# Time mixing in one fixed TensorE order, with the substitution recorded later and the receptance multiplied early

## The chip, the cores and the metric

The kernel runs on one core of a Trainium2 chip. The metric is the device time of one execution in microseconds (us). Each stated time is the median of several runs; beside it stands one profiled execution, from which all rows below come. TensorE (PE) does matrix products and transposes, VectorE (DVE), ScalarE (ACT) and GpSimd (POOL) do the rest, and SyncE (SP) issues the loads of the weights. Each engine works through its own queue in order; semaphores tie the queues together.

## The reference, cut to what matters

The reference is two blocks of two layers each, on 256 tokens of width 1024 in float32. The first block (sparse, latent and forgetting attention, a cross attention and an MLP in each layer) is not touched. A layer of the second block is, cut to its core:

```python
h = rms_norm_2(x, norm_g) * (1.0 + scale) + shift
proj = h @ w_in
pool_u, pool_g, q, k, v, ret_g, rw, rw_g, gate_logits = jnp.split(proj, points, axis=-1)
o_pool = causal_pool_mixer(pool_u, pool_w, pool_scale) * jax.nn.silu(pool_g)
o_ret = retention(q, k, v, positions, ret_norm_g) * jax.nn.silu(ret_g)
o_rwkv = rwkv7_time_mix(rw, ...) * jax.nn.silu(rw_g)
y = jnp.einsum('btnw,nwd->btnd', stack(o_pool, o_ret, o_rwkv), w_branch)
x = x + gate * (jnp.sum(jax.nn.sigmoid(gate_logits) * y, axis=2) @ w_out)
```

In rwkv7_time_mix the projected features are first shifted, p + (p_prev - p) * mu, and then each of eight heads runs a recurrence over the tokens, in which a state of 64 x 64 is multiplied by a decay and corrected by two outer products (time mixing). retention rotates q and k (rotary positions), takes masked and decayed scores in chunks of 128 tokens, and normalises each head.

## The kernel before, in words

A layer of the second block is the function `block2_layer`, called twice; layer 0 begins at about 928 us of the span and layer 1 at about 1281 us. The weights `w_in_2` are cut into chunks of 512 columns. A chunk comes as four loads (tile `raw`, four buffers, issued by SyncE at L76); each is split into a high half `hi` (ScalarE, L112) and a low half `lo` (VectorE, L113), and a raw buffer is free when its low half is done. A gemm does three products for each pair of operand and weight (L138, L139, L140). `gemm_b` writes features by tokens, 24 matmuls of 256 columns for each 128 features; `gemm_a` writes tokens by features with 512 columns.

The stage of time mixing, in the order of the code:

- With the operand that is not yet normalised (`xop`, 258 columns), the low-rank input and the keys `kT` are multiplied (chunk 0); `mixed_unscaled` puts the norm and the token shift in afterwards. Then `hop`, the normalised operand, is made.
- The decays (L1070 to L1085), the squares of the keys (ACT, L1089), their sums by head (PE, L1095), and `kn`, a power on GpSimd (L1098).
- The receptance `rT` (chunk 1) with `hop`, in the function `shifted`; the exponentials `Ei`, `En`, `Ee` out of matmuls at L1106; `Bt` and its companions on VectorE (L1131 to L1144).
- The values `vT` (chunk 2), then masked products (`masked`, L1154, copied by a mask at L1157) into `LT`, which GpSimd writes to memory (`lt`) and reads back as `band`, a 16 x 16 block for each of 128 rows.
- The substitution (L1185, L1186): fifteen products and fifteen reduces on VectorE, which solve these blocks into `zb`; a DMA from GpSimd's queue writes them to memory (`zd`, L1187).
- `bonus`, then `rotated(4)` and `rotated(3)`, the retention's keys `rk_` and queries `rq` (chunks 4 and 3). Each is two gemms of 48 matmuls, and for each of its four pieces two copies on ScalarE into `row` (three buffers, L1382, L1383), a product with the cosine on VectorE (L1386), and a product with the sine and an addition on GpSimd (L1384, L1387).
- The retention's values `rv` (chunk 5), `inverse_parts` (four loads of `zd` into `TT` from GpSimd's queue, L1195), `silu_gate` for chunk 6 into `kT` (L1369, L1370), the retention's scores (PE L1412 and L1417, VectorE L1414 and L1420) and its output (PE L1429, L1432).
- `recurrence` (it inverts the blocks, L1202, and solves) interleaved with `other_branches`, which are the pooling branch, the remaining gates and one of the branch gates.

Outside of two sections with a manual schedule for PE, a scheduler sets the order of an engine's instructions from the order in which they are recorded and from their dependences. Inside such a section (L1515) TensorE's order is that of the code. The generators `recurrence` and `other_branches` are advanced by turns there, so that each yield is a place at which the other's matmuls go in. PSUM tiles have tags with fixed numbers of banks: "mm" four, "s" two, "t" and "o" one each. `bt("gt", ...)` has four buffers, "P" and "PT" four; `raw_load` takes a raw buffer, `aux` a "gt" buffer.

Of the kernel before, what the change touches and what calls it, by code (L numbers as in the profile page):

```python
# [42 lines left out]
def program(ctx: ExitStack, tc: tile.TileContext, T: dict, out: bass.AP):  # L43
# [939 lines left out]
    def block2_layer(l, x, r, us, K, xop):  # L983
# [61 lines left out]
        for j in range(4):  # L1045
            mixed_unscaled(kT[:, j, :], ups[1 + j], 1 + j)

# [52 lines left out]
        us = chunk_b(1)  # L1100
        shifted(1, rT, us)
# [73 lines left out]
        zb = bt("PT", [128, 31, 16])  # L1175
        pool.memset(zb, 0.0)
        pool.memset(zb[:, 15:31, 0:1], 1.0)
        tmp = bt("dg", [128, 256])
        zrow = zb[:, 15:31, :]
        for i in range(14, -1, -1):  # L1180
            m = 15 - i
            zv = bass.AP(tensor=zrow.tensor, offset=zrow.offset + 16 * i + 15 + 1,
                         ap=[list(zrow.ap[0]), [1, m], [15, m]])
            tv = tmp[:, :m * m].rearrange("p (a b) -> p a b", b=m)
            ver.tensor_mul(out=tv, in0=zv, in1=band[:, i, 1:m + 1].unsqueeze(1).broadcast_to([128, m, m]))  # L1185
            ver.reduce_sum(out=zrow[:, i, 1:m + 1], in_=tv, axis=AX.X)  # L1186
        pool.dma_start(out=flat(K["zd"], 16, *blocks), in_=zrow)  # L1187

# [45 lines left out]
        def bonus():  # L1234

            for n in range(2):
                p = pst("t")
                for ct in range(4):
                    pe.transpose(p[:, 128 * ct:128 * ct + 128], vT[:, ct, tok(n)], ident)
                ver.tensor_copy(out=Vn[:, n, :], in_=p)  # L1240
            for c2 in range(2):
                p = pst("s")
                for i in range(2):
                    pe.matmul(p[:, 256 * i:256 * i + 256], lhsT=K["bones"], rhs=kT[:, 2 * c2 + i, :],
                              start=True, stop=True)
                ver.tensor_mul(out=flat2(vT[:, 2 * c2:2 * c2 + 2, :]), in0=p, in1=flat2(vT[:, 2 * c2:2 * c2 + 2, :]))

        def by_token():
            BK = bt("aT", [128, 2, 512])
            for i, src in enumerate((Bt, Kt)):  # L1250
                p = pst("t")
                for ct in range(4):
                    pe.transpose(p[:, 128 * ct:128 * ct + 128], src[:, ct, 0:128], ident)
                act.copy(out=BK[:, i], in_=p)
            return BK[:, 0], BK[:, 1]
# [134 lines left out]
        bonus()  # L1390
        rk_ = rotated(4)
        pool.tensor_mul(out=Ei, in0=Ei, in1=rT)

        rq = rotated(3)
        rv = bt("gt", [128, 2, 512])
        us = chunk(5)
        o = [pst("mm"), pst("mm")]
        gemm_a(o, hop, us)
        for t in range(2):
            ver.tensor_copy(out=rv[:, t, :], in_=o[t])  # L1400

        inverse_parts()
        oop = Op([None, None, None])
        sg = {}

        def retention_scores():
            dm = raw_load(T["ret_decay"]).rearrange("p (h t) -> p h t", t=256)
            sc0 = bt("gt", [128, 4, 256])
# [10 lines left out]
            sc1 = bt("gt", [128, 4, 128])  # L1419
# [30 lines left out]
        def other_branches(on):  # L1450
# [21 lines left out]
            w0 = raw_load(T["pool_band"][0]).rearrange("p (g t) -> p g t", t=256)  # L1472
# [24 lines left out]
            th[0, 0] = bt("gt", [128, 4, 256])  # L1497
            yield from gate_tanh(th[0, 0], 0, 0)
# [12 lines left out]
        sg[6] = bt("kT", [128, 4, 256])  # L1511
        for _ in silu_gate(sg[6], 6):
            pass
        on = retention_out(*retention_scores())
        with tc.manual_schedule(engines={mybir.EngineType.PE}):  # L1515
            others = other_branches(on)
            for _ in recurrence():
# [368 lines left out]
```

## Time and profile before

| what | value |
| --- | --- |
| median of 3 runs | 1629.22 us (1626.84 to 1631.49) |
| profiled execution | 1626.35 us |
| its span | 1624.6 us |
| mean granted TensorE clock | 0.979 |
| TensorE busy | 1555.3 us, 96% |
| VectorE, ScalarE, GpSimd busy | 1104.6, 741.3, 252.3 us |

The profiled execution lies 2.9 us under the median. A row of busy time counts an engine as busy from an instruction's start to its end, and matmuls overlap. A wait is idle time of an engine and is put down to the instruction that ended it. [...]

### The profile page before, as it was taken

Reading aid. Unit: us, or ns where it says so; the run is one execution under the profiler, and the core shown is the slowest. Engines: PE = TensorE matmul, PEld = TensorE weight load, DVE = VectorE, ACT = ScalarE, POOL = GpSimd, SP = SyncE. Lnnn points to the kernel's source line nnn. Section 1 sums busy time; section 2 is a strip of 40 time slices with the busy share of each in tenths; the row PEclk is TensorE's granted clock in tenths of the full one; section 3 lists DMA queues with packets and bytes.
Section 4 is the critical chain, followed back from the end, with each engine's and each line's share of the span. In section 5 each row is a group of like instructions: output and inputs, shape, how many; then the busy total and the mean of one; then the engine's idle time right before and its main releaser. Section 6 shows DMA issues by size and latency. Waiting matters only on the chain.

```text
span 1624.6 us, 29823 instructions
## 1 busy us (share of the span) xinstructions
PE 1555.3 (96%) x12106; PEld 1433.0 (88%) x12106; DVE 1104.6 (68%) x1773; ACT 741.3 (46%) x1190; POOL 252.3 (16%) x247
## 2 busy tenths in 40 slices
PE   7999999999999999998999999899999999899998
PEld 6789997899879899987999789789999889799997
DVE  5476568866776766689876777765565786664754
ACT  4666344544445664454544364423443654233441
POOL 1000110111100001101111132311111313101202
PEclk9899999999999999999999989999999999999999
DMA  8733465687776234664788645624365346432552
GB/s 294 256 105 114 159 230 173 201 274 256 259 254 207 93 105 155 209 211 144 257 274 269 215 134 160 196 85 132 104 183 181 104 159 175 148 130 79 176 184 69
DMA packets 81033, 288.98 MB, mean 178 GB/s; under 512 B 9224, under 2 KB 10304, under 8 KB 80896
## 3 DMA queue, kind: packets, MB, share of 16 engines
q1 hardware_dynamic: 78768, 280.07, 52.6%
q0 software_dynamic: 2128, 7.01, 1.5%
q8 instruction: 95, 1.56, 0.4%
q14 instruction: 42, 0.34, 0.1%
HBM read 281.48 MB, written 5.55 MB: 177 GB/s over the span
## 4 chain that ended last, share of the span: by engine, by line
PE 42%; DVE 6%; DMA 2%; ACT 2%; issue 2%; POOL 1%; DVEq 0%; POOLq 0%; ACTq 0%
PE mm L138 10%; PE mm L139 10%; PE mm L140 10%; DVE lo L113 2%; PE s L138 2%; PE s L139 2%; PE s L140 2%; DMA raw<-in_w_in 1%; PE s L1154 1%; ACT hi L112 1%; PE o L1270 1%; PE t L1270 1%; PE o L1301 1%; PE t L1202 1%; PE s L1202 0%
## 5 line engine op out<-in xcount | busy, mean ns | idle before, releaser
L113 DVE TENSOR_TENSOR lo<-raw,hi 128x1024 fp32r<-128x1024 f32 (+1 forms) x429 | 545.6, 1279 | 258.1 <-ACT hi L112 256.1
L112 ACT CAST hi<-raw 128x1024 fp32r<-128x1024 f32 (+1 forms) x435 | 453.0, 1048 | 518.8 <-PE mm L139 238.0
L138 PE MATMUL mm<-act,hi 128*128 128x256 f32 x1808 | 522.2, 289 | 2.0 <-DVE act L130 2.0
L139 PE MATMUL mm<-act,hi 128*128 128x256 f32 x1808 | 514.2, 285 | 0.5 <-DVE act L128 0.5
L140 PE MATMUL mm<-act,lo 128*128 128x256 f32 x1808 | 513.6, 285 | 0.0
L138 PEld LDWEIGHTS mm<-act,hi 128*128 128x128 f32 x1808 | 348.5, 193 | 8.8 <-issue 4.3
L139 PEld LDWEIGHTS mm<-act,hi 128*128 128x128 f32 x1808 | 348.4, 193 | 1.9 <-DVE act L128 0.9
L140 PEld LDWEIGHTS mm<-act,lo 128*128 128x128 f32 x1808 | 347.7, 193 | 0.5 <-issue 0.2
L138 PE MATMUL mm<-hi,act 128*128 128x512 f32 (+1 forms) x320 | 126.2, 395 | 5.4 <-ACT hi L127 5.2
L138 PE MATMUL s<-act,hi 128*128 128x256 f32 x448 | 127.8, 285 | 3.3 <-DVE P L128 1.7
L140 PE MATMUL s<-act,lo 128*128 128x256 f32 x448 | 127.5, 285 | 0.0
L139 PE MATMUL s<-act,hi 128*128 128x256 f32 x448 | 127.5, 285 | 0.0
L140 PE MATMUL mm<-hi,act 128*128 128x512 f32 (+1 forms) x320 | 123.8, 387 | 3.0 <-DVE act L128 3.0
L139 PE MATMUL mm<-lo,act 128*128 128x512 f32 (+1 forms) x320 | 123.6, 386 | 0.4 <-DVE lo L113 0.4
L138 PEld LDWEIGHTS s<-act,hi 128*128 128x128 f32 x448 | 86.7, 194 | 4.4 <-DVE P L128 2.2
L139 PEld LDWEIGHTS s<-act,hi 128*128 128x128 f32 x448 | 86.6, 193 | 0.2
L140 PEld LDWEIGHTS s<-act,lo 128*128 128x128 f32 x448 | 86.7, 194 | 0.0
L138 PEld LDWEIGHTS mm<-hi,act 128*128 128x128 f32 x320 | 61.4, 192 | 18.1 <-ACT hi L127 5.2
L1623 DVE CUSTOM_DVE_ANT_0 raw<-raw,gt 128x1024 f32<-128x1024 f32 x48 | 59.9, 1253 | 25.4 <-DMA raw<-in_w_ada 25.3
L140 PEld LDWEIGHTS mm<-hi,act 128*128 128x128 f32 x320 | 61.2, 191 | 17.0 <-DVE act L128 4.3
L138 PE MATMUL mm<-hi,P 128*128 128x512 f32 x192 | 74.8, 389 | 0.0
L139 PE MATMUL mm<-lo,P 128*128 128x512 f32 x192 | 74.8, 389 | 0.0
(509 smaller groups left out, 2324.8 us busy)
## 6 DMA issues: line engine op xcount, KB each, us to landing
raw<-in_w_in SPq DMA_DIRECT2D x119, 512.0 KB, 4.6
raw<-in_w_up SPq DMA_DIRECT2D x64, 512.0 KB, 4.6
raw<-in_w_down SPq DMA_DIRECT2D x64, 512.0 KB, 4.6
raw<-in_w_gate SPq DMA_DIRECT2D x48, 512.0 KB, 3.5
raw<-in_w_ada SPq DMA_DIRECT2D x48, 512.0 KB, 4.4
raw<-in_w_gl SPq DMA_DIRECT2D x48, 512.0 KB, 3.5
raw<-in_w_branch SPq DMA_DIRECT2D x24, 512.0 KB, 3.4
raw<-in_w_br SPq DMA_DIRECT2D x16, 512.0 KB, 3.4
```

Of the source, the lines that this page charges most:

```text
L112: act.copy(out=h[:, :cols], in_=r[:, :cols])
L113: (eng or ver).tensor_sub(out=l[:, :cols], in0=r[:, :cols], in1=h.bitcast(F32)[:, :cols])
L138: pe.matmul(o, lhsT=lh, rhs=rh, start=first, stop=False)
L139: pe.matmul(o, lhsT=lh, rhs=rl, start=False, stop=False)
L140: pe.matmul(o, lhsT=ll, rhs=rh, start=False, stop=last)
L1154: pe.matmul(p[par][:, 128 * ct:128 * ct + 128], lhsT=lm[pp, ct, cs], rhs=rm[pp, ct, cs], start=True, stop=True)
L1202: pe.matmul(p[half(a), 64 * i:64 * i + 64], lhsT=lhs(i, a), rhs=rhs(i, a), start=True, stop=True)
L1270: pe.matmul(p[par][:, 64 * ct:64 * ct + 64], lhsT=m[par][:, ct, :], rhs=v(par, ct), start=first and ct == 0, stop=last and ct == 3, skip_g ...
L1301: pe.matmul(p[half(a), col_of(par, ct)], lhsT=TT[n][half(a), 4 * par + ct, :], rhs=x0[half(a), col_of(par, ct)], start=True, stop=True)
L1623: ver.tensor_tensor_reduce(out=r, in0=r, in1=box["c"], scale=1.0, scalar=0.0, op0=ALU.mult, op1=ALU.add, accum_out=mods[l][:, o:o + 1])
```

## The change

First, the receptance's gemm (chunk 1) is moved up behind the keys' gemm and uses the operand `xop`; `mixed_unscaled` finishes it at the old place. Second, the manual section begins earlier: it now holds `rv`, `bonus`, `rotated(4)`, the substitution, `rotated(3)`, `inverse_parts`, the gate of chunk 6 in two halves around the scores, the retention's output, four steps of `other_branches`, and only then the recurrence. `other_branches` ends with three branch gates instead of one; the two later ones used to follow the section. Third, the transposes in `bonus` and `by_token` alternate between the banks "t" and "o", the copies of `Vn` go to ScalarE, and `ret_decay` and the first half of `pool_band` come through `aux`.

```diff
@@ -1044,6 +1044,11 @@
             mixed_unscaled(kT[:, j, :], ups[1 + j], 1 + j)
+        us = chunk_b(1)
+        ups = []
+        for j in range(4):
+            ups.append(pst("mm"))
+            gemm_b(ups[j][:, 0:258], xop, us, 128 * j)
...
@@ -1097,8 +1102,8 @@
-        us = chunk_b(1)
-        shifted(1, rT, us)
+        for j in range(4):
+            mixed_unscaled(rT[:, j, :], ups[j], 5 + j)
...
@@ -1172,20 +1177,6 @@
         pool.dma_start(out=band, in_=flat(K["lt"], 0, *blocks))
-        zb = bt("PT", [128, 31, 16])
...
-        pool.dma_start(out=flat(K["zd"], 16, *blocks), in_=zrow)
...
@@ -1234,10 +1225,10 @@
-                p = pst("t")
+                p = pst("to"[n])
...
-                ver.tensor_copy(out=Vn[:, n, :], in_=p)
+                act.copy(out=Vn[:, n, :], in_=p)
...
@@ -1387,25 +1378,11 @@
-        bonus()
-        rk_ = rotated(4)
-        pool.tensor_mul(out=Ei, in0=Ei, in1=rT)
-
-        rq = rotated(3)
-        rv = bt("gt", [128, 2, 512])
...
-        inverse_parts()
...
-            dm = raw_load(T["ret_decay"]).rearrange("p (h t) -> p h t", t=256)
-            sc0 = bt("gt", [128, 4, 256])
+            sc0 = bt("P", [128, 4, 256])
...
@@ -1494,8 +1471,9 @@
-            th[0, 0] = bt("gt", [128, 4, 256])
-            yield from gate_tanh(th[0, 0], 0, 0)
+            for br in range(3):
+                th[0, br] = bt("gt", [128, 4, 256])
+                yield from gate_tanh(th[0, br], 0, br)
...
@@ -1508,12 +1486,43 @@
-        sg[6] = bt("kT", [128, 4, 256])
-        for _ in silu_gate(sg[6], 6):
-            pass
-        on = retention_out(*retention_scores())
         with tc.manual_schedule(engines={mybir.EngineType.PE}):
+            rv = bt("gt", [128, 2, 512])
+            us = chunk(5)
+            o = [pst("mm"), pst("mm")]
+            gemm_a(o, hop, us)
+            for t in range(2):
+                ver.tensor_copy(out=rv[:, t, :], in_=o[t])
+            bonus()
+            rk_ = rotated(4)
+            pool.tensor_mul(out=Ei, in0=Ei, in1=rT)
+            zb = bt("PT", [128, 31, 16])
...
+            pool.dma_start(out=flat(K["zd"], 16, *blocks), in_=zrow)
+            rq = rotated(3)
+            dm = aux(T["ret_decay"]).rearrange("p (h t) -> p h t", t=256)
+            inverse_parts()
+            sg[6] = bt("kT", [128, 4, 256])
+            gate = silu_gate(sg[6], 6)
+            for _ in range(2):
+                next(gate)
+            scs = retention_scores()
+            for _ in gate:
+                pass
+            on = retention_out(*scs)
             others = other_branches(on)
+            for _ in range(4):
+                next(others)
             for _ in recurrence():
                 next(others, None)
```

In the orders below each line of the kernel keeps its own number, so that one statement has two: L1384 and L1387 (the two GpSimd pieces of `rotated`) are L1375 and L1378 in the changed kernel, L1382 and L1383 (its copies) L1373 and L1374, L1187 (zd) L1511, L1195 (TT) L1186, L1412 and L1417 (scores) L1389 and L1394, L1095 L1100, L1106 L1111, L1154 L1159, L1343 L1334.

The queue of GpSimd around zd in layer 0, before; the last two products and additions belong to the second half of rq:

```order
L1384 TENSOR_TENSOR row_10622<-row_10622,sin 128x256
L1387 TENSOR_TENSOR gt_10566<-gt_10566,row_10622 128x256
L1187 DMA zd<-PT_10335 2048x1x16
L1384 TENSOR_TENSOR row_10677<-row_10677,sin 128x256
L1195 DMA TT_10370<-zd 64x8x64
L1387 TENSOR_TENSOR gt_10566<-gt_10566,row_10677 128x256
L1384 TENSOR_TENSOR row_10683<-row_10683,sin 128x256
L1195 DMA TT_10370<-zd 64x8x64
L1387 TENSOR_TENSOR gt_10566<-gt_10566,row_10683 128x256
L1195 DMA TT_10371<-zd 64x8x64 x2
```

The same place in the changed kernel, where gt_10665 is rq:

```order
L1378 TENSOR_TENSOR gt_10482<-gt_10482,row_10599 128x256
L1511 DMA zd<-PT_10606 2048x1x16
L1186 DMA TT_10355<-zd 64x8x64
L1375 TENSOR_TENSOR row_10715<-row_10715,sin 128x256
L1186 DMA TT_10355<-zd 64x8x64
L1378 TENSOR_TENSOR gt_10665<-gt_10665,row_10715 128x256
L1375 TENSOR_TENSOR row_10721<-row_10721,sin 128x256
L1186 DMA TT_10356<-zd 64x8x64
L1378 TENSOR_TENSOR gt_10665<-gt_10665,row_10721 128x256
L1186 DMA TT_10356<-zd 64x8x64
L1375 TENSOR_TENSOR row_10776<-row_10776,sin 128x256
L1378 TENSOR_TENSOR gt_10665<-gt_10665,row_10776 128x256
```

All eight pieces of rq now stand behind zd and the first TT load, where three stood behind the first TT load before.

ScalarE's queue in layer 1, before, from rq's last copies (row) to the casts of gate 6 (hi_2462 and later; hi_2433 and hi_2436 are rv's):

```order
L1382 COPY row_2408_14405<-mm_2407_14356 64x256
L1383 COPY row_2408_14405<-mm_2407_14356 64x256
L1382 COPY row_2409_14411<-mm_2407_14356 64x256
L1383 COPY row_2409_14411<-mm_2407_14356 64x256
L112 CAST hi_2433_14513<-raw_2432_14511 128x1024
L112 CAST hi_2436_14519<-raw_2435_14517 128x1024
L112 CAST hi_2462_14736<-raw_2461_14734 128x1024
L112 CAST hi_2465_14742<-raw_2464_14740 128x1024
L112 CAST hi_2468_14748<-raw_2467_14746 128x1024
```

The same place in the changed kernel, where hi_2444 to hi_2453 are the four units of gate 6:

```order
L1373 COPY row_2437_14469<-mm_2435_14414 64x256
L1374 COPY row_2437_14469<-mm_2435_14414 64x256
L112 CAST hi_2444_14545<-raw_2443_14543 128x1024
L1373 COPY row_2439_14524<-mm_2438_14475 64x256
L1374 COPY row_2439_14524<-mm_2438_14475 64x256
L112 CAST hi_2447_14551<-raw_2446_14549 128x1024
L1373 COPY row_2440_14530<-mm_2438_14475 64x256
L1374 COPY row_2440_14530<-mm_2438_14475 64x256
L112 CAST hi_2450_14557<-raw_2449_14555 128x1024
L112 CAST hi_2453_14563<-raw_2452_14561 128x1024
```

The casts of gate 6 now stand between and behind the last copies of rq; row_2439 takes the buffer of row_2419, the last of rk's four rows, whose sine product and addition on GpSimd stand behind a TT load.

TensorE's queue in layer 1, before, at the scores, from the last matmuls of rv's and gate 6's gemms on (here the second half of gate 6, mm_2439, and then the retention's output):

```order
L138 MATMUL mm_2439_14574<-act_2292_13629,hi_2436_14519 128x256
L139 MATMUL mm_2439_14574<-act_2293_13630,hi_2436_14519 128x256
L140 MATMUL mm_2439_14574<-act_2292_13629,lo_2437_14520 128x256
L1412 MATMUL mm_2442_14628<-gt_2403_14294,gt_2384_14146 128x256 x2
L1412 MATMUL mm_2443_14632<-gt_2403_14294,gt_2384_14146 128x256 x2
L1417 MATMUL mm_2444_14636<-gt_2403_14294,gt_2384_14146 128x128 x4
L1429 MATMUL mm_2447_14644<-gt_2410_14417,gt_2441_14627 128x128 x4
```

The same place in the changed kernel, where mm_2455 is the first half of gate 6 and mm_2461 the second:

```order
L138 MATMUL mm_2455_14567<-act_2316_13773,hi_2447_14551 128x256
L139 MATMUL mm_2455_14567<-act_2317_13774,hi_2447_14551 128x256
L140 MATMUL mm_2455_14567<-act_2316_13773,lo_2448_14552 128x256
L1389 MATMUL mm_2457_14617<-gt_2434_14413,gt_2413_14230 128x256 x2
L1389 MATMUL mm_2458_14621<-gt_2434_14413,gt_2413_14230 128x256 x2
L1394 MATMUL mm_2459_14625<-gt_2434_14413,gt_2413_14230 128x128 x4
L138 MATMUL mm_2461_14634<-act_2314_13771,hi_2450_14557 128x256
L139 MATMUL mm_2461_14634<-act_2315_13772,hi_2450_14557 128x256
```

The scores now stand between the two halves of gate 6, 48 matmuls behind rq's gemm; before, rv's gemm and the whole of gate 6 stood between.

## Rows read from the trace of the kernel before

**Rows 1.** The page, busy time of each engine over the whole span.

```profile
PE 1555.3 (96%) x12106; PEld 1433.0 (88%) x12106; DVE 1104.6 (68%) x1773; ACT 741.3 (46%) x1190; POOL 252.3 (16%) x247
```

**Rows 2.** Waits of PE from 928 us on: total us, times, longest.

```profile
engine line waited for: us in total, times, longest us
PE mm L1417 <- DVE kT L1370: 8.9, 2, 5.1
PE t L1343 <- DVE PT L1336: 3.9, 2, 1.9
PE t L1239 <- DVE vT L1006: 2.2, 3, 1.1
...
PE mm L1429 <- DVE gt L1414: 2.2, 1, 2.2
PE t L1095 <- ACT P L1089: 2.1, 1, 2.1
```

**Rows 3.** Busy time and granted clock (PEclk) of five stretches.

```profile
core 0: us, PE busy (x) PEld busy (x) DVE busy (x) ACT busy (x) POOL busy (x), PEclk, DMA share, GB/s
956.60:966.80 10.20, 10.20 (x36) 8.15 (x36) 6.45 (x10) 7.10 (x12) 3.16 (x2) 0.50 0.24 67
...
1052.10:1059.00 6.90, 5.07 (x22) 4.79 (x23) 5.73 (x13) 1.54 (x2) 0.00 (x0) 0.51 0.64 208
...
1390.20:1396.90 6.70, 5.22 (x22) 4.91 (x23) 6.64 (x12) 2.59 (x3) 0.00 (x0) 0.50 0.65 201
...
1161.40:1164.80 3.40, 3.40 (x18) 3.40 (x17) 1.30 (x1) 2.39 (x6) 2.19 (x1) 0.50 0.00 0
...
1295.00:1305.00 10.00, 9.93 (x61) 7.80 (x60) 8.72 (x20) 6.88 (x15) 3.64 (x3) 1.00 0.04 6
```

**Rows 4.** PE in order of time: first matmuls of rv and gate 6, scores, tail.

```profile
start us, us, engine line op out<-in xcount [idle before <-releaser]
1022.51 0.40 PE L138 MATMUL mm<-hi,act 128*128 128x512 f32 x1
...
1160.36 0.63 PE L1343 MATMUL t<-cpack,PT 128*128 128x128 f32 x4 [1.93 <-DVE PT L1336]
...
1361.77 0.40 PE L138 MATMUL mm<-hi,act 128*128 128x512 f32 x1
...
1372.68 0.28 PE L138 MATMUL mm<-act,hi 128*128 128x256 f32 x1
...
1384.52 1.97 PE L1412 MATMUL mm<-gt,gt 128*128 128x256 f32 x8 [0.17 <-DVE gt L1400]
```

**Rows 5.** Waits of SP's DMA queue, 1335 to 1400 us: total us, times, longest.

```profile
SPq L76 <- DVE PT L1186: 16.2, 2, 11.1
```

**Rows 6.** POOL in order of time, layer 0, columns as in rows 4.

```profile
1031.09 1.13 POOL L1187 DMA_DIRECT2D zd<-PT  x1 [0.17 <-issue]
...
1039.87 0.72 POOL L1195 DMA_DIRECT2D TT<-zd  x1 [6.13 <-DMA zd<-PT]
1040.59 0.76 POOL L1387 TENSOR_TENSOR gt<-gt,row 128x256 f32<-128x256 f32 x1
```

**Rows 7.** DVE in order of time, layer 0: masked copies, substitution, low half, splitting.

```profile
998.40 1.34 DVE L1157 COPY_PREDICATED P<-masks,s 128x512 f32<-128x512 uint8 x2
...
1012.10 0.16 DVE L1185 TENSOR_TENSOR dg<-PT,dg 128x1 f32<-128x1 f32 x1 [5.45 <-DMA dg<-lt]
...
1030.40 0.39 DVE L1186 TENSOR_REDUCE PT<-dg 128x15 f32<-128x225 f32 x1
...
1042.10 1.23 DVE L113 TENSOR_TENSOR lo<-raw,hi 128x1024 fp32r<-128x1024 f32 x1 [4.33 <-ACT hi L112]
...
1168.97 1.23 DVE L131 SCALAR_TENSOR_TENSOR act<-rT,act 128x1024 fp32r<-128x1024 f32 x1
```

**Rows 8.** POOL in order of time, layer 1.

```profile
1363.80 1.55 POOL L1384 TENSOR_TENSOR row<-row,sin 128x256 f32<-128x256 f32 x1 [1.20 <-ACT row L1383]
...
1370.05 1.14 POOL L1187 DMA_DIRECT2D zd<-PT  x1 [0.28 <-issue]
1379.11 0.72 POOL L1195 DMA_DIRECT2D TT<-zd  x1 [7.92 <-DMA zd<-PT]
```

**Rows 9.** ACT in order of time, layer 1: a cast of gate 6.

```profile
1385.01 1.05 ACT L112 CAST hi<-raw 128x1024 fp32r<-128x1024 f32 x1 [1.12 <-DMA raw<-in_w_in]
```

More of the change, by code (lines that the diff above doesn't have):

```diff
@@ L1174, in block2_layer @@
         pool.dma_start(out=band, in_=flat(K["lt"], 0, *blocks))
-        zb = bt("PT", [128, 31, 16])
[L1176 to L1186, printed above, removed]
-        pool.dma_start(out=flat(K["zd"], 16, *blocks), in_=zrow)
         TT = [bt("TT", [128, 8, 64]) for n in range(2)]
@@ L1250, in by_token @@
             for i, src in enumerate((Bt, Kt)):
-                p = pst("t")
+                p = pst("to"[i])
                 for ct in range(4):
@@ L1388, in rotated @@
             return dst
-        bonus()
-        rk_ = rotated(4)
-        pool.tensor_mul(out=Ei, in0=Ei, in1=rT)
-        rq = rotated(3)
-        rv = bt("gt", [128, 2, 512])
[L1396 to L1400, printed above, removed]
-        inverse_parts()
         oop = Op([None, None, None])
@@ L1418, in retention_scores @@
                           start=True, stop=True)
-            sc1 = bt("gt", [128, 4, 128])
+            sc1 = bt("PT", [128, 4, 128])
             ver.tensor_mul(out=sc1, in0=p.rearrange("p (a b) -> p a b", b=128), in1=dm[:, :, 0:128])
@@ L1471, in other_branches @@
                     yield
-            w0 = raw_load(T["pool_band"][0]).rearrange("p (g t) -> p g t", t=256)
+            w0 = aux(T["pool_band"][0]).rearrange("p (g t) -> p g t", t=256)
             w1 = raw_load(T["pool_band"][1])[:, 0:512].rearrange("p (g t) -> p g t", t=128)
@@ L1509, in gate_tanh @@
                 act.activation(out=flat2(tt[:, j:j + 2, :]), in_=p, func=AF.Tanh, scale=0.5)
-        sg[6] = bt("kT", [128, 4, 256])
-        for _ in silu_gate(sg[6], 6):
-            pass
-        on = retention_out(*retention_scores())
         with tc.manual_schedule(engines={mybir.EngineType.PE}):
+            rv = bt("gt", [128, 2, 512])
[8 more added lines that the diff above has]
+            zb = bt("PT", [128, 31, 16])
+            pool.memset(zb, 0.0)
+            pool.memset(zb[:, 15:31, 0:1], 1.0)
+            tmp = bt("dg", [128, 256])
+            zrow = zb[:, 15:31, :]
+            for i in range(14, -1, -1):
+                m = 15 - i
+                zv = bass.AP(tensor=zrow.tensor, offset=zrow.offset + 16 * i + 15 + 1,
+                             ap=[list(zrow.ap[0]), [1, m], [15, m]])
+                tv = tmp[:, :m * m].rearrange("p (a b) -> p a b", b=m)
+                ver.tensor_mul(out=tv, in0=zv, in1=band[:, i, 1:m + 1].unsqueeze(1).broadcast_to([128, m, m]))
+                ver.reduce_sum(out=zrow[:, i, 1:m + 1], in_=tv, axis=AX.X)
+            pool.dma_start(out=flat(K["zd"], 16, *blocks), in_=zrow)
[10 more added lines that the diff above has]
+            on = retention_out(*scs)
             others = other_branches(on)
+            for _ in range(4):
+                next(others)
             for _ in recurrence():
```

## The prediction

> **What bounds the kernel now.** I read the busy times first, then the list of what TensorE waited for, then the granted clock of the stretches behind the waits, and last the order of time on the engines that release TensorE. TensorE is busy 96% of the span [rows 1], and the change leaves its matmuls what they are. So what can be won is the idle time of TensorE and the stretches at half clock, and both only in the second block, from 928 us on, where the changed function runs twice (layer 0, then layer 1). Here is what is lost there now:
>
> - Ahead of L1095, once, 2.1 us: the squares of the keys (ACT, L1089) come late [rows 2]. Behind it 10.2 us run at clock 0.50 with TensorE busy throughout [rows 3]. [...] In layer 1 there is no such wait, and the same lines run at clock 1.00 [rows 3].
> - L1239 behind vT: 2.2 us, of which 1.4 in layer 1 [rows 2].
> - L1417 waits for gate 6 (kT): 8.9 us in two waits, 5.1 of it in layer 1, so 3.8 in layer 0; L1429 2.2 us in layer 0 [rows 2]. Behind them the clock is 0.51 and 0.50, with 5.1 and 5.2 us of busy time [rows 3]: 2.5 and 2.6 us lost. The source is the order on VectorE. SyncE's weight loads wait 16.2 us in layer 1 for the substitution's reduces, because the low halves (L113) that free the four raw buffers are queued behind them [rows 5]; ScalarE's cast of gate 6 then waits for the landing [rows 9], kT is late, and TensorE stands the 5.1 us.
> - L1343 waits 3.9 us in two waits [rows 2], with 3.4 us at clock 0.50 behind one of them [rows 3], 1.7 us lost each time.
>
> In sum 2.1 + 5.1 + 0.8 + 3.8 + 2.2 + 2.5 + 1.9 + 1.7 = 20.1 us in layer 0 and 1.4 + 5.1 + 2.6 + 2.0 + 1.7 = 12.8 us in layer 1.
>
> **The change, part by part.**
>
> *Receptance early.* Its four gemms of 24 matmuls stay the same work (258 columns instead of 256). Ahead of L1100 (old L1095) they put some 11.5 us of TensorE work, since a chunk of 96 such matmuls takes as long as gate 6 does, 1372.7 to 1384.4 [rows 4]. The missing squares need 2.1 us: the wait goes, and with it the fall of the clock, 7.2 us in layer 0 and nothing in layer 1. In exchange the exponentials' matmuls (L1111) lose the cover of this gemm, and eight of them come with few gemm matmuls between. I charge 1.0 us in each layer; from below that is 0, from above the 2.1 us of the wait that goes. VectorE gets eight small operations more and GpSimd four; they lie under the gemm.
>
> *Substitution after rotated(4).* On VectorE the low halves of rk now stand ahead of the substitution, and those of the first half of gate 6 get their raw buffers from them. The late weights behind L1417 go, and with them what stands at L1417 and L1429 with its clock. But zd's DMA now stands ahead of all GpSimd work of rq (layer 0), or ahead of that and the second half of rk's (layer 1), and the TT loads are queued right behind it; each L1375 and L1378 of rq stands behind a TT load that waits for zd. Before, four of rq's eight pieces were done when zd was issued in layer 0, and rv's gemm of 10.9 us and gate 6's 11.6 us [rows 4] stood between rq and its first reader, L1412. Now the first reader, L1389, stands half a gate behind rq, 5.8 us. This is the price of the change.
>
> *Layer 0 step by step.* The masked copies ended at 999.7 and the substitution began at 1012.1 [rows 7]. With 7.2 us won, 1.0 lost and six rv matmuls now ahead of L1159 they end about 5 us sooner, so the substitution begins at 1007. It took 18.7 us, to 1030.8 [rows 7], with other work between; with less of that I take 17, to 1024. zd was issued at 1031.1 and GpSimd went on at 1039.9 [rows 6]: 8.8 us, so TT starts at 1032.8. Then follow four TT issues of 0.7 us and eight pieces of 0.75 us [rows 6], 8.8 us, to 1041.6. TensorE finished rq at 1022.5 [rows 4]; less 7.2 + 0.8 us, plus 10.9 of rv, that is 1025.4, and with 0.4 of the new small waits about 1026. VectorE is still in the substitution then, so gate 6's low half comes some 1.3 us late, and TensorE stands at L1389 at 1033 instead of going on. It ends L1389 at 1042, of which about 0.5 is work: a wait of 8.5 to 9 us, take 9. Behind it the clock will be at half as behind L1417 now: 2.5 us. Sum of the new costs: 1.0 + 1.3 + 9 + 2.5 = 13.8 us.
>
> *Layer 1 step by step.* Nothing is won ahead of the masks, so the substitution begins at 1352 and ends at 1370 as before (its zd was issued at 1370.1 and let GpSimd go on at 1379.1 [rows 8]). After that come TT, the last L1375 of rk, TT and its L1378, 2.9 us, to 1382. For that L1378 waits the third copy of rq (L1373, it takes over the buffer of rk's last row), and behind this copy on ScalarE stands the cast of the second weight unit of gate 6: two copies, a cast of 1.05 us [rows 9], a low half of 1.2 us [rows 7], to 1384.4 and 1385.6. TensorE finished rq at 1361.8 [rows 4]; less 1.4, plus 10.9 and 1.0, that is 1372.3, and after twelve matmuls of gate 6, at 1373.7, it stands: 10.7 to 11 us. Behind it the remaining 36 matmuls run at half clock, 2.5 us. GpSimd's last piece of rq ends about 1390, under these. Sum: 1.0 + 11 + 2.5 = 14.5 us.
>
> *The tail.* Ahead of L1334 (old L1343) stand 48 gate matmuls where 30 stood; at 0.12 us each (11.6 us for 96 [rows 4]) that is 2.2 us more cover against waits of 1.9 and 2.0 us: the wait goes with its clock, 3.6 us in each layer. What is late next is the branch gemm that needs yT; two gate halves and two branch gemms, 11.5 us, lie between, and the chain through the addition and the splitting took 9.2 us (1161.0 to 1170.2 [rows 4, 7]). I charge nothing; without that cover it would be 1 to 3 us.
>
> *Alternating banks and copies on ScalarE, decay by the other pool.* Small waits of the order of 0.7 us (bonus, by_token) go, 1.4 us in all.
>
> Sum: 20.1 + 12.8 + 1.4 - 13.8 - 14.5 = 6.0 us won. The profiled execution took 1626.35 us, so 1620.3; the median of the runs shown lies 2.9 us above the profiled execution, so **1623 us**, 0.4% faster.
>
> [...] zd takes 8.8 us from issue to GpSimd's release in layer 0 and 9.0 in layer 1 [rows 6, 8]. [...]
>
> **Rivals.**
> - *Short wait for zd.* [...] Chance 0.12. [...]
> - *The queue costs nothing*, as GpSimd is through with rq's pieces before TensorE asks. Then 31 us are won (34.3 less the small waits): 1598 us. The order on GpSimd and the landings speak against it. Chance 0.12.
> - *The clock behind the masks falls anyway*, because the small matmuls at L1075 to L1100 draw it down without any wait. Then the 5.1 us stay: 1628 us, no change. Layer 1's clock of 1.00 at these lines [rows 3] speaks against it. Chance 0.14.
> - *Slower: GpSimd's pieces stretched.* The pieces that stand behind zd take 0.75 us when VectorE is idle or slow, but 1.55 us in the one row here that stands beside its work [rows 8], and it will work: it does the low halves that had to wait. Sixteen pieces at 1.55 are 12.8 us more, and the clock then stays low as long as the longest stretch seen, 10.2 us, 2.5 us more in each layer: 1623 + 17.8 = 1641 us. It turns the sign from a mean piece of about 1.1 us on (6 us over sixteen pieces). Against it: most rows show 0.74 to 0.76. Chance 0.14.
>
> **How the numbers follow.** My forecast has 0.48; around it the wait for zd and the start of the substitution are uncertain by some 3 us in each layer, so it spreads over 1615 to 1631. About 0.3% (4.9 us) is what a measurement of this kernel can tell from no change. Faster: 0.31 of the forecast's 0.48, the first two rivals' 0.24, 0.02 of the third: 0.57. Slower: 0.13 of the last, 0.01 of the forecast and 0.02 of the third: 0.16. Same: the rest, 0.27. The range, 1600 to 1636, leaves out most of the 1598 and 1641 cases.
>
> **What would show it.** Right: no wait at L1100, clock 1.0 at 955 to 970, GpSimd still for 6 to 8 us ahead of the first TT load in both layers, TensorE waiting about 9 us at L1389 in layer 0 and about 11 us at the second weight unit of gate 6 (released by the cast) in layer 1, nothing at L1334. Wrong: a wait of less than 4 us in either place, TensorE waiting over 3 us at L1111 or at the branch gemm, or a clock below 1 behind L1075.

## The result and the profile after

The changed kernel takes 1617.54 us (median of 6 runs, 1615.14 to 1623.85) against 1629.15 us (6 runs, 1626.78 to 1631.49): a ratio of 0.9943, with an interval of 0.9921 to 0.9965. It is faster by 0.6%. The forecast was 1623, its range 1600 to 1636. The profiled execution took 1615.78 us (before 1626.35), its span is 1613.7 us (before 1624.6) and its mean granted clock 0.983 (before 0.979).

The span is 10.9 us shorter. Measured between the starts of the waits at L356 and at L1023, layer 0 went from 355.97 to 347.86 us, 8.1 less; from there to the end, layer 1 went from 339.58 to 338.03, 1.5 less. The remaining 1.2 us lie in the first block, which has the same code; the six runs of the changed kernel lie up to 8.7 us apart.

The busy times answer to [rows 1]; TensorE is busy 6.1 us less, though it does the same 12106 matmuls, because at a mean granted clock of 0.983 instead of 0.979 fewer of them ran at half clock:

```profile
PE 1549.2 (96%) x12106; PEld 1428.4 (89%) x12106; DVE 1101.8 (68%) x1785; ACT 742.8 (46%) x1194; POOL 260.0 (16%) x255
```

What TensorE waited for from 926 us on (total us, times, longest), against [rows 2]. The waits at L1095, L1239, L1343, L1417 and L1429 have no successor; these rows are new but the last, which was at 0.4 us (L1154):

```profile
PE mm L138 <- ACT hi L112: 5.2, 3, 4.1
PE mm L1389 <- POOL gt L1378: 4.6, 2, 2.9
PE mm L140 <- DVE lo L113: 3.4, 3, 1.9
...
PE s L1159 <- DVE LT L1162: 1.8, 2, 1.5
...
PE s L1159 <- DVE Bt L1142: 1.5, 1, 1.5
```

Busy time and granted clock of five stretches, columns as in [rows 3]:

```profile
955.00:968.80 13.80, 13.80 (x93) 11.51 (x92) 11.23 (x27) 9.20 (x16) 4.86 (x7) 1.00 0.49 176
968.90:972.20 3.30, 3.30 (x11) 2.85 (x12) 1.12 (x3) 2.15 (x4) 2.14 (x2) 0.50 0.46 159
1040.60:1047.30 6.70, 5.00 (x21) 4.61 (x21) 4.17 (x7) 2.09 (x2) 1.78 (x2) 0.50 0.49 153
1303.40:1310.10 6.70, 6.70 (x19) 5.12 (x18) 1.67 (x3) 3.20 (x8) 2.15 (x1) 0.50 0.42 151
1371.70:1378.40 6.70, 3.94 (x16) 3.64 (x17) 6.06 (x5) 4.50 (x6) 6.53 (x7) 0.50 0.43 127
```

The third and the fifth stretch stand behind the waits at L1389 and in gate 6, as foreseen. The second and the fourth do not: at 968.9 and 1303.4 TensorE is busy for the whole stretch, 3.30 of 3.30 and 6.70 of 6.70 us, and has not stood still ahead of it (no idle time over 0.15 us between 934 and 987 us, nor between 1278 and 1326), yet the granted clock is 0.50, half of full speed.

GpSimd in layer 0 from zd on (start, duration, idle time before), against [rows 6]:

```profile
1023.78 1.12 POOL L1511 DMA_DIRECT2D zd<-PT  x1
1031.48 0.72 POOL L1186 DMA_DIRECT2D TT<-zd  x1 [6.59 <-DMA zd<-PT]
...
1037.05 1.27 POOL L1375 TENSOR_TENSOR row<-row,sin 128x256 f32<-128x256 f32 x1
1038.39 1.59 POOL L1378 TENSOR_TENSOR gt<-gt,row 128x256 f32<-128x256 f32 x1
1039.95 1.71 POOL L1375 TENSOR_TENSOR row<-row,sin 128x256 f32<-128x256 f32 x1
1041.73 0.72 POOL L1378 TENSOR_TENSOR gt<-gt,row 128x256 f32<-128x256 f32 x1
```

TensorE at the scores in the same place, against [rows 4]:

```profile
1035.76 1.42 PE L1389 MATMUL mm<-gt,gt 128*128 128x256 f32 x4
1040.04 0.77 PE L1389 MATMUL mm<-gt,gt 128*128 128x256 f32 x2 [2.87 <-POOL gt L1378]
1042.51 1.22 PE L1389 MATMUL mm<-gt,gt 128*128 128x256 f32 x2 [1.71 <-POOL gt L1378]
```

The third piece of rq ends at 1038.39 + 1.59 = 1039.98 and lets the fifth matmul go at 1040.04; the last ends at 1042.45 and lets the seventh go at 1042.51. The first four found their pieces ready.

In layer 1 the chain runs from zd over GpSimd, ScalarE's copy and cast to TensorE, as foreseen. GpSimd first ([rows 8]), then ScalarE ([rows 9]), then TensorE:

```profile
1361.16 1.14 POOL L1511 DMA_DIRECT2D zd<-PT  x1 [0.61 <-DVE gt L1377]
...
1367.84 0.72 POOL L1186 DMA_DIRECT2D TT<-zd  x1 [3.96 <-DMA zd<-PT]
...
1369.94 0.74 POOL L1378 TENSOR_TENSOR gt<-gt,row 128x256 f32<-128x256 f32 x1
```

```profile
1370.71 0.37 ACT L1373 COPY row<-mm 64x256 f32<-64x256 f32 x1 [4.98 <-POOL gt L1378]
...
1371.48 1.04 ACT L112 CAST hi<-raw 128x1024 fp32r<-128x1024 f32 x1
```

```profile
1372.58 0.58 PE L138 MATMUL mm<-act,hi 128*128 128x256 f32 x1 [4.09 <-ACT hi L112]
...
1375.26 0.58 PE L140 MATMUL mm<-act,lo 128*128 128x256 f32 x1 [1.88 <-DVE lo L113]
```

TT goes at 1367.84, rk's last addition ends at 1370.68, the copy that takes over its row buffer starts at 1370.71, the cast behind the copy ends at 1372.52, and TensorE goes on at 1372.58.

### The profile page after: what moved, and what is told of

Read it like the earlier page. It is cut to its first block, busy times and chain, and to the rows that moved or that the text cites. A ratio compares the mean times of both kernels' runs of the same rounds, so it can differ in the third digit from the quotient of the medians.

```text
span 1613.7 us, 29837 instructions
## 1 busy us (share of the span) xinstructions
PE 1549.2 (96%) x12106; PEld 1428.4 (89%) x12106; DVE 1101.8 (68%) x1785; ACT 742.8 (46%) x1194; POOL 260.0 (16%) x255
## 4 chain that ended last, share of the span: by engine, by line
PE 42%; DVE 6%; DMA 2%; issue 2%; POOL 1%; ACT 1%; DVEq 0%; POOLq 0%; ACTq 0%; SPq 0%
PE mm L138 10%; PE mm L140 10%; PE mm L139 10%; DVE lo L113 2%; PE s L138 2%; PE s L140 2%; PE s L139 2%; DMA zd<-PT 1%; PE s L1159 1%; PE o L1261 1%; PE s L1111 1%; PE t L1261 1%; PE o L1292 1%; ACT hi L112 1%; PE t L1193 1%
## 5 line engine op out<-in xcount | busy, mean ns | idle before, releaser
L113 DVE TENSOR_TENSOR lo<-raw,hi 128x1024 fp32r<-128x1024 f32 (+1 forms) x429 | 545.1, 1278 | 226.0 <-ACT hi L112 224.6
L138 PE MATMUL mm<-act,hi 128*128 128x256 f32 x1744 | 504.6, 289 | 7.2 <-ACT hi L112 5.2
L140 PE MATMUL mm<-act,lo 128*128 128x256 f32 x1744 | 496.7, 285 | 3.4 <-DVE lo L113 3.4
L139 PE MATMUL mm<-act,hi 128*128 128x256 f32 x1744 | 495.6, 284 | 0.5 <-DVE act L128 0.5
L138 PEld LDWEIGHTS mm<-act,hi 128*128 128x128 f32 x1744 | 335.6, 192 | 15.4 <-ACT hi L112 5.8
L140 PEld LDWEIGHTS mm<-act,lo 128*128 128x128 f32 x1744 | 335.2, 192 | 5.6 <-DVE lo L113 4.3
L139 PEld LDWEIGHTS mm<-act,hi 128*128 128x128 f32 x1744 | 335.4, 192 | 1.7 <-DVE act L128 0.9
```

What stands on the lines that cost most here:

```text
L113: (eng or ver).tensor_sub(out=l[:, :cols], in0=r[:, :cols], in1=h.bitcast(F32)[:, :cols])
L138: pe.matmul(o, lhsT=lh, rhs=rh, start=first, stop=False)
L139: pe.matmul(o, lhsT=lh, rhs=rl, start=False, stop=False)
L140: pe.matmul(o, lhsT=ll, rhs=rh, start=False, stop=last)
```

## The experiments

Times are medians. Kernels of one group ran on one chip with runs of the kernel before beside them; ratios are to those.

### TT behind rq

The theory: what the changed order costs comes from GpSimd's queue, where rq's pieces stand behind TT loads that wait for zd. The four loads are made to follow the last addition of rq; TensorE's order stays.

```diff
+        last_add = []
...
-                    pool.tensor_add(out=dv, in0=dv, in1=sw)
+                    last_add[:] = [pool.tensor_add(out=dv, in0=dv, in1=sw).ins]
...
-            inverse_parts()
+            with tc.issue_after(last_add[0]):
+                inverse_parts()
```

> The changed kernel with one edit: the four TT loads are issued behind rq's last addition on GpSimd, instead of among rq's pieces. Nothing else moves. Theory (what is left of the change's price is GpSimd's queue standing at zd's landing): the waits at L1389 (4.6 us, layer 0) and at gate 6's second weight unit (4.1 + 1.9 us, layer 1) go, and with them the two stretches of 6.8 us at half clock behind them (about 2.5 and 2 us); TT lands some 5 us later than in the changed kernel, still 15 us ahead of L1193. About 14 us under the changed kernel, near 1603 us. Rival (these waits come from VectorE, which is in the substitution until just before, or from weights that land late): the waits stay within 1 us of what they are and the time within 3 us of 1617.5.

Measured: 1606.49 us, ratio 0.9862 (0.9831 to 0.9892); on another chip 1604.88 us, 0.9870 (0.9849 to 0.9891). TensorE's waits for the casts, for GpSimd and for the low halves were 5.2 + 4.6 + 3.4 = 13.2 us in the changed kernel; here they are:

```profile
PE mm L140 <- DVE lo L113: 2.6, 3, 1.1
...
PE mm L1391 <- POOL gt L1380: 0.8, 1, 0.8
...
PE mm L138 <- ACT hi L112: 0.5, 1, 0.5
```

So 9.3 us of waiting go, and the stretches at half clock at 1040 and 1371 us with them (in the profile on the other chip two of 3.4 us remain there). The theory holds: the queue behind zd was the main price of the change, and what the change wins elsewhere does not need it.

### The receptance early, alone

The kernel before with only the first part of the change.

```diff
+        us = chunk_b(1)
+        ups = []
+        for j in range(4):
+            ups.append(pst("mm"))
+            gemm_b(ups[j][:, 0:258], xop, us, 128 * j)
...
-        us = chunk_b(1)
-        shifted(1, rT, us)
+        for j in range(4):
+            mixed_unscaled(rT[:, j, :], ups[j], 5 + j)
```

> The kernel before with the first part of the change alone: the receptance's gemm early, with the unscaled operand. Theory: the wait of 2.1 us at L1095 in layer 0 goes; the stretch at half clock behind it shrinks from 10.2 us to 3.4 (as in the changed kernel) or to none; in layer 1 a stretch of 6.8 us at half clock may come in, as in the changed kernel, since the small matmuls now stand together. So 5.5 us won in layer 0, 0 to 3.4 lost in layer 1: 1623.5 to 1627 us. Rival (the later waits for gate 6 are set by the loads and not by TensorE, and take the gain back): 1628 to 1630 us, with L1417's two waits grown by the amount won ahead of them.

Measured: 1627.07 us (12 runs) against 1627.41, ratio 0.9999 (0.9977 to 1.0020): no gain. The wait for the squares is gone from the list, but the clock falls all the same, in layer 0 for as long as before and in layer 1 for the first time, with TensorE busy throughout:

```profile
967.60:977.70 10.10, 10.10 (x34) 8.32 (x34) 3.71 (x6) 4.47 (x12) 3.28 (x2) 0.50 0.28 88
1312.40:1319.10 6.70, 6.70 (x19) 5.05 (x19) 0.91 (x2) 3.23 (x8) 1.39 (x1) 0.50 0.22 80
```

This is the profile of the slowest of the twelve runs (1633.59 us, mean clock 0.973), so its stretches can be longer than in most. In it, of the 7.2 us only the 2.1 us of the wait were to be won in layer 0, and layer 1 lost 3.4 us. The late gate at L1417 (8.9 us [rows 2]) stays, at 8.2 us, and the wait behind it, at the old L1429, grows from 2.2 to 4.1 us. So a part of the rival holds as well.

### The change without it

The reverse diff: the changed kernel with the receptance's gemm back behind `kn`, with `hop`.

> The changed kernel without its first part: the receptance's gemm stays at its old place, with the normalised operand. Theory: the wait for the squares of the keys comes back in layer 0 with its stretch of 10.2 us at half clock (about 5.5 us), and in layer 1 the stretch of 6.8 us at half clock behind L1100 goes (3.4 us won): 1618 to 1621 us. Rival (the parts need each other, so that without the early gemm all waits of zd grow): above 1624 us.

Measured: 1623.8 us (12 runs), ratio 0.9970 (0.9952 to 0.9989). The time lies between the two expectations. Without this part the rest wins 0.3%; with it 0.6%, though alone it wins nothing; the intervals leave open whether the parts add up. The wait for the squares is back, and that for gate 6's casts is longer than the 5.2 us of the changed kernel:

```profile
PE mm L138 <- ACT hi L112: 9.1, 3, 4.7
...
PE t L1095 <- ACT P L1089: 2.0, 1, 2.0
```

But the wait at the scores is gone from the list, and with the low halves' 4.2 us the waits for casts, GpSimd and low halves come to 13.3 us, against 13.2 in the changed kernel. So it is not there that the two kernels differ, but at the squares, in the wait and in the clock behind it:

```profile
957.20:970.50 13.30, 13.30 (x48) 10.51 (x47) 8.26 (x12) 8.44 (x13) 3.72 (x2) 0.50 0.30 93
1290.00:1312.00 22.00, 21.94 (x161) 19.80 (x160) 18.97 (x35) 14.99 (x27) 4.28 (x4) 1.00 0.41 126
```

In layer 0 half clock lasts 13.3 us, against 3.3 in the changed kernel; in layer 1 the clock stays at 1.00 where the changed kernel has 6.7 us at 0.50. Without the early receptance layer 1 doesn't fall there, neither here nor before the change [rows 3]; with it alone it does.

### The substitution recorded first

The changed kernel with the substitution and zd recorded at their old place, behind `band`.

> The changed kernel with the substitution recorded at its old place, ahead of rv, rather than behind rotated(4); the TensorE order stays fixed as in the change. Theory: on VectorE the low halves of rk and rq then stand behind the substitution's steps, which wait for the band; weights come late at rk or rq, TensorE waits there for 3 to 8 us in each layer and longer at half clock, while zd lands 1 to 4 us sooner: 1620 to 1632 us. Rival (the fixed order alone brings the gain, and where the substitution is recorded is indifferent): 1615 to 1620 us.

Measured: 1617.49 us (12 runs), ratio 0.9944 (0.9922 to 0.9967), the changed kernel's time. The rival holds. The wait only changes its form, more of it at the scores (here L1402) than at the casts:

```profile
PE mm L1402 <- POOL gt L1391: 6.7, 3, 4.0
PE mm L138 <- ACT hi L112: 4.1, 2, 3.7
```

So the place of the substitution in the code isn't what the change wins by.

### One branch gate inside, as before

```diff
-            for br in range(3):
-                th[0, br] = bt("gt", [128, 4, 256])
-                yield from gate_tanh(th[0, br], 0, br)
+            th[0, 0] = bt("gt", [128, 4, 256])
+            yield from gate_tanh(th[0, 0], 0, 0)
```

> The changed kernel with the tail part undone: other_branches ends with one branch gate again, the two others follow the section. Theory (the tail term of the prediction: a wait of 1.9 to 2.0 us at L1334 and 1.7 us of half clock behind it come back in each layer): 3.6 us per layer, so about 7 us over the changed kernel's 1617.5, 1623 to 1626. Rival (the wait at the tail was only one of many places where TensorE idles, and without it the same idle time shows at the branch gemm or in the next layer's start): within 2 us of 1617.5. The list of waits of TensorE tells them apart: two waits of about 2 us at L1334 by the theory, none or shorter ones by the rival.

Measured: 1623.87 us (12 runs), ratio 0.9973 (0.9958 to 0.9987): 0.3 percentage points over the changed kernel's ratio, 4.9 us. The wait at L1334 is back, but smaller than the 3.9 us of [rows 2]:

```profile
PE t L1334 <- DVE PT L1327: 1.7, 2, 0.8
```

From the wait at L1261 to the last gemm's wait for its split operand (L130) this profile is 1.23 and 3.05 us longer than the changed kernel's, 4.3 us together. That holds the 1.7 us of the two waits and, in layer 1, 1.7 us for a stretch of 3.4 us at half clock at 1470 us, ahead of L1334; whether this edit causes that stretch is not shown. The other 4.0 us of its longer span (1622.0 us) go with more half clock at 968, 1282 and 1306 us (6.8, 3.4 and 10.2 us, against 3.3, none and 6.7), at places which this edit doesn't touch. The theory's sign holds; of its 7 us the profile shows at most 4.3 at the tail.

### One bank

The changed kernel with `bonus` and `by_token` on the bank "t" alone and the copies of `Vn` on VectorE.

```diff
-                p = pst("to"[n])
+                p = pst("t")
...
-                act.copy(out=Vn[:, n, :], in_=p)
+                ver.tensor_copy(out=Vn[:, n, :], in_=p)
```

> The changed kernel with the alternating banks and the copies on ScalarE undone: bonus and by_token take the bank t alone and Vn is copied by VectorE. Theory (prediction: 1.4 us in all): the wait at L1230 behind the copy comes back as two or three waits of about 1 us, 1618 to 1620. Rival (in the new order VectorE is in the substitution's neighbourhood when bonus runs, so that a copy on it comes later, and TensorE, whose order is now fixed, stands for it): over 1622, with a wait of more than 3 us at L1230.

Measured: 1626.72 us (12 runs), ratio 0.9991 (0.9976 to 1.0005). The rival holds: without this part, charged with 1.4 us, nearly all of the gain in the new order is gone. TensorE's waits, then VectorE in order of time in layer 1:

```profile
PE t L1230 <- DVE PT L1510: 6.7, 1, 6.7
...
PE t L1230 <- DVE P L1231: 3.2, 1, 3.2
```

```profile
1345.53 0.16 DVE L1509 TENSOR_TENSOR dg<-PT,dg 128x1 f32<-128x1 f32 x1 [3.66 <-DMA dg<-lt]
...
1347.13 1.28 DVE L1495 COPY gt<-mm 128x512 f32<-128x512 f32 x2
1348.33 0.68 DVE L1231 COPY P<-t 128x512 f32<-128x512 f32 x1
```

The copy that frees the bank (L1231) ends at 1349.01, and TensorE, which had stood since 1342.39, goes on at 1349.07; the list names the short reduce that VectorE does just behind the copy. Ahead of the copy VectorE's queue holds the first product of the substitution, which itself stands 3.66 us for `band` to arrive. In the fixed order nothing else on TensorE went past in these 6.7 us. The 9.9 us are not all lost: the waits for the casts and at the scores, 9.8 us in the changed kernel, are 1.1 us here, and this profile, of the fastest of the twelve runs, is 6.5 us longer than the changed kernel's. The edit undoes the banks and the copies together; which of them matters more is not separated.

### The masks under the values

The kernel with TT behind rq, in which the masked products and the writing and reading of `lt` are recorded between rv's four weight units.

> The kernel of the experiment with TT behind rq (1606.5), in which in addition the masked products, the writes and the reading of lt and the band are recorded between the four weight units of rv, so that TensorE has rv's matmuls to do while Bt and LT are made. Theory: the waits of L1159 for Bt and LT, 3.3 us over the two layers in that kernel, go, and nothing takes their place: 1602 to 1604. Rival: the substitution now begins later by the matmuls that stand ahead of the masks, zd comes later, and the wait turns up at inverse_parts' first reader or at gate 6 again: 1606 or more, with a wait of TensorE for POOL or for a low half behind L1389.

Measured: 1609.27 us, ratio 0.9883 (0.9863 to 0.9902), no better than without. Of the waits at L1159 one is left, and the scores wait again, because zd is now issued at 1033.5 instead of 1024.3 us in layer 0, and rq's pieces stand behind it in GpSimd's queue:

```profile
PE mm L1381 <- POOL gt L1370: 3.2, 2, 1.6
...
PE s L1159 <- DVE LT L1162: 1.5, 1, 1.5
```

The rival holds.

### Squares between the halves of the receptance

What draws the clock down at 969 and 1303 us with TensorE busy? The squares, their sums (16 matmuls of 2 columns, L1100) and `kn` are moved between the two halves of the early receptance gemm, away from the small matmuls of the decays and exponentials. The set-up of the constants, which only layer 0 runs, moves up with them. The edit was run on three kernels: with the masks moved, with TT behind rq, and on the changed kernel.

```diff
-        for j in range(4):
+        for j in range(2):
             ups.append(pst("mm"))
             gemm_b(ups[j][:, 0:258], xop, us, 128 * j)
+        sq = bt("P", [128, 4, 256])
...
+        pool.tensor_tensor(out=kn, in0=kn, in1=mhalf, op=ALU.pow)
+        for j in range(2, 4):
...
```

> The kernel with TT behind rq and the masks between rv's weight units, in which in addition the squares of the keys, their sums at L1100 and kn stand between the two halves of the early receptance gemm, so that the sums' small matmuls and those of the exponentials no longer follow one another closely. Theory (the falls of the clock to 0.50 at L1100 to L1111, 6.8 us of them in each layer with TensorE busy throughout, come from small matmuls standing close together): the falls between 955 and 975 and between 1295 and 1312 shrink from 6.8 us to 3.4 or nothing, and the time is 1.7 to 3.4 us per layer under the same kernel without this. Rival (the falls come from something else, the exponentials' fp32 matmuls themselves or the chip's state, whatever stands ahead of them): the same falls of 6.8 us, and the time within 2 us of the kernel without it.

> TT behind rq (1606.5 in its first runs), with the squares, their sums and kn between the two halves of the early receptance gemm; the masks stay where the changed kernel has them. Theory (the falls of the clock at 966 and 1301 us come from the sums' two-column matmuls standing next to the decays' and the exponentials' small ones; in the experiment with the masks moved too they were gone): 3.4 us less per layer, 1599 to 1602, and no stretch at 0.50 between 955 and 980 or between 1295 and 1312. Rival (the gain of that experiment over the masks alone, 5 us, came from the masks' later place, since kn was ready sooner): 1605 to 1608, with the falls still there or with a longer wait at L1159 for LT.

> The changed kernel itself with the squares, their sums and kn between the two halves of the early receptance gemm, and nothing else. Theory: the falls at 968.9 (3.4 us) and 1303.4 (6.8 us) go, 1.7 + 3.4 = 5.1 us, 1611 to 1614. Rival (what TensorE wins there it waits longer for zd behind, since the substitution still ends when VectorE and the memory let it): 1616 to 1618, with longer waits at L1389 and at gate 6.

> The kernel with TT behind rq once more, on the chip of the two others, as their measure. Both theories: within 3 us of its 1606.5; falls of the clock of 3.4 to 6.8 us at L1100 to L1111 in both layers, as in its first profile. If the falls are absent here, they come and go from run to run and the two others say nothing about their cause.

| kernel | without the edit | with it |
| --- | --- | --- |
| masks moved | 1609.27, 0.9883 | 1603.99, 0.9853 (0.9831 to 0.9875) |
| TT behind rq | 1604.88, 0.9870 | 1602.29, 0.9861 (0.9838 to 0.9884) |
| the changed kernel | 1617.54, 0.9943 | 1611.66, 0.9913 (0.9890 to 0.9936) |

TT behind rq without the edit, two stretches:

```profile
968.50:971.80 3.30, 3.30 (x11) 2.47 (x10) 1.66 (x3) 1.61 (x4) 2.68 (x2) 0.50 0.39 137
1299.50:1306.30 6.80, 6.80 (x20) 5.16 (x19) 1.64 (x3) 3.13 (x8) 2.12 (x1) 0.50 0.41 154
```

The same kernel with the edit:

```profile
955.00:972.00 17.00, 16.58 (x117) 14.48 (x116) 16.11 (x34) 14.05 (x23) 7.22 (x7) 1.00 0.64 202
1290.00:1307.00 17.00, 16.91 (x104) 13.84 (x103) 12.21 (x25) 11.22 (x25) 7.33 (x7) 1.00 0.56 186
```

In all three profiles with the edit the clock is 1.00 there in both layers. Eight profiles have the early receptance without the edit: the changed kernel, TT behind rq twice, the receptance alone, the substitution first, one branch gate, one bank and the masks moved. In layer 0 the clock falls there in all eight, for 3.3 to 10.1 us; in layer 1 it falls in seven. The exception is the kernel with the masks moved, which in layer 1 keeps 1.00 with the same small matmuls together:

```profile
970.00:980.10 10.10, 10.10 (x34) 8.32 (x35) 3.71 (x6) 4.52 (x12) 3.28 (x2) 0.50 0.27 86
1290.00:1312.00 22.00, 21.87 (x152) 19.35 (x151) 17.56 (x38) 15.49 (x30) 6.79 (x6) 1.00 0.48 158
```

So where the sums stand with the other small matmuls, the clock falls in fifteen of sixteen cases, and where they are moved away, in none of six, with no wait of TensorE ahead of the falls. That this grouping draws the clock down is shown by these counts; what decides in the one case that kept its clock, and what it is in the group that counts, is not.

The time says less. Put at half their length, an estimate, the stretches cost (3.3 + 6.8) / 2 = 5.1 us; the three pairs differ by 2.6 to 5.9 us in medians. No one interval tells its pair apart, but the three agree in sign. Other things differ too: the two profiles of TT behind rq are of the slowest run without the edit and of the fastest with it, and on the changed kernel, whose two times come from different groups, the waits for casts, GpSimd and low halves go from 13.2 to 8.7 us. So the rival of longer waits for zd does not hold there. The best kernel of the study is TT behind rq with this edit, 1602.29 us.

## Why the forecast came out, step by step

Right in the sign and the range; two large terms were too high, one was missed, and these partly cancel. The two are the 9 us at L1389, 4.4 too high, and the 11 us in gate 6 of layer 1, 3.7 too high, 8.1 together; the one missed is half clock at the early receptance, 1.7 and 3.4 us, 5.1 together. That the sum came as near as it did is in part luck.

| term | forecast us | profile after us |
| --- | --- | --- |
| L1100's wait and its clock, layer 0 | 7.2 won | 7.2 won, but 3.3 at half clock behind: 1.7 lost |
| the same lines, layer 1 | nothing | 6.7 at half clock: 3.4 lost |
| small waits | 1.0 lost a layer | at L1159: 1.8 less 0.4 of before; 1.5 |
| gate 6's low half, layer 0 | 1.3 lost | 0.55 + 0.76 = 1.3 lost |
| L1389, layer 0 | 9 lost | 2.87 + 1.71 = 4.6 lost |
| gate 6, layer 1 | 11 lost | 0.58 + 0.76 + 4.09 + 1.88 = 7.3 lost |
| half clock behind these | 2.5 and 2.5 lost | 2.5 and 2.0 lost |
| old L1417, L1429, L1343, L1239 | won | won, no successor |

With these the new costs are 11.5 us in layer 0 (forecast 13.8) and 14.2 in layer 1 (14.5). Add the stretch of 3.4 us at half clock behind L1023 that the profile of before shows at 1287.7 us and this one doesn't, 1.7 us, and the forecast's 6.0 become 10.3 us, with the first block's 1.2 us 11.5; the span shows 10.9.

- *Receptance early.* This step failed, and a clock below 1 behind L1075, which came in both layers, was on the forecast's own list of what would show it wrong. It read the fall of the clock behind L1095 as the wait's doing, since layer 1, which had no wait, showed 1.00 [rows 3]. But the wait went and the fall stayed. The third rival had the mechanism for the new order: the small matmuls draw the clock down. Layer 1 kept full clock in both profiles without the early receptance and lost it with that part alone, so it is this part that brought the fall there. The rival's price, 5.1 us, was too high for layer 0 (1.7), and it named nothing for layer 1 (3.4); that the two make 5.1 as well is chance. How much of the old fall in layer 0 was the wait's doing and how much the small matmuls', no run separates. The forecast's 5.1 us are half of the 10.2 us at 0.50 [rows 3], and the losses in the table are put the same way: an estimate, and no run shows the half. Up to the start of the next instruction, four decay matmuls took 2.00 us at 0.50 (L1081, kernel before, from 959.90 us on) and 1.05 us at 1.00 (L1086, changed kernel, from 964.71 us on); gate 6's matmuls of 256 columns started 0.21 us apart at 0.50 (from 1375.64 us on) and 0.12 us apart at 1.00 (from 1383.81 us on). By these a stretch costs an estimated 0.44 to 0.48 of its length, 4.5 to 4.9 us for 10.2.
- *The queue behind zd.* Place and chain were right in both layers, down to the cast that releases TensorE in layer 1; the experiment with TT behind rq shows that it is the cause. Both sizes were too high, for different reasons. In layer 0 the last piece ended at 1042.45 (forecast 1041.6), 2.1 us later when the 1.2 us of the first block are added, but TensorE came to L1389 at 1035.76 instead of 1033, by the same count 4.0 us later; the half clock at 969 us and the waits at L1159 explain 2.1 us of that beyond the 1.0 charged, and the rest stays open. Its first four matmuls, 1.42 us, found rq's first pieces ready; the forecast let the whole of L1389 wait. In layer 1 zd let GpSimd go after 1367.84 - 1361.16 = 6.7 us, where 9.0 were taken from before.
- *The landing of zd.* From its issue to the first TT load it took 7.7 and 6.7 us here; over all runs in which TT waits for it, 6.0 to 9.1 us. The rival of the short wait, with its chance of 0.12, held in none: no run shows a wait below 6.0 us.
- *GpSimd's pieces stretched.* Pieces of 1.27 to 1.72 us did come, three of rq's eight in layer 0 and four in layer 1; the mean of the sixteen is 1.1 us, the point from which this rival was to turn the sign. It did not, because those of layer 1 lay beside gate 6, where L1389 did not wait, and those of layer 0 (2.3 us more than at 0.75) are within the 4.6 us at L1389.
- *The tail.* No wait at L1334 and no wait of the branch gemms, as forecast; undoing it costs at most 4.3 us in one profile where 7.2 were forecast, and the waits that come back are 0.8 us each where 1.9 and 2.0 stood before.
- *Banks and copies.* The waits at L1239 (2.2 us, in the two sums of what is lost) and at L1253 (1.4 us, as charged) are gone. But the step looked only at what goes; the experiment with one bank shows that without it the fixed order would have cost 9.9 us at L1230, and 6.5 us of the span with the waits that shrink in return.

## What to carry to other kernels

When TensorE's order is written by hand, look at every queue that feeds it for a DMA that waits on memory or on a late producer: here rq's pieces stood behind a TT load that came after 6.6 us of idle time in layer 0 and 4.0 in layer 1. Moving the DMA behind the work that TensorE needs next (here four loads, 11 us by the medians) was worth as much as the whole reordering. A copy that frees a PSUM bank should not go on an engine whose queue stands still at that moment, as VectorE's did here for 3.66 us in front of the substitution, with TensorE waiting 6.7 us at L1230. And before a fall of the clock is put down to a wait, look at which matmuls run in it: here TensorE was busy throughout, hiding the wait did not bring the clock back (10.1 us at 0.50 with the receptance early alone), and moving the two-column matmuls between large ones did (1.00 in three profiles).

## What the runs showed of the hardware

The clock fell with TensorE busy without a gap, where 2-column sums, decays and exponentials stood together (6.70 of 6.70 us busy at 0.50), in fifteen of sixteen cases. TensorE had no wait ahead of these falls.

The time of one kernel moves with the mean clock granted in a run: 29 runs of the kernel before on one chip lie between 1619.5 us at 0.985 and 1636.6 us at 0.972. A stretch of 3.4 us at half clock behind L1023 is in one of the two profiles of TT behind rq and not in the other. One profile therefore can't settle a term of 2 us.

GpSimd and VectorE were slower side by side. While the pieces in layer 0 took 1.27 to 1.71 us instead of 0.74 to 0.76, three low halves on VectorE took 4.82 us, 1.61 each instead of 1.23 [rows 7]:

```profile
1036.25 4.82 DVE L113 TENSOR_TENSOR lo<-raw,hi 128x1024 fp32r<-128x1024 f32 x3 [0.65 <-ACT hi L112]
```

If nothing at all overlapped, a pair would take an estimated 0.75 + 1.23 = 1.98 us; the pairs took 1.6 to 1.7. What slows them is not shown.
